# The second feed-forward's way down as seven block products, with tokens on the partitions

## The chip, the cores and the metric

The kernel is one decoder layer in float32 on one core of a Trainium2 chip. The metric is the device time of one execution in microseconds (us). The engines are named as in the profile: PE (TensorE: matrix products into the accumulator banks), PEld (its weight loads, which overlap the products), DVE (VectorE), ACT (ScalarE), POOL (GpSimd) and SP (SyncE, here only an issuer of transfers). Every engine takes its instructions in one fixed order, and a transfer issued from ACT or POOL stands in that engine's order too.

## The reference, cut to what matters

```python
def swiglu(h, w_gu, w_down):
    gu = h @ w_gu
    g, u = jnp.split(gu, 2, axis=-1)
    return (jax.nn.silu(g) * u) @ w_down          # the product this case is about
...
    f = swiglu(rmsnorm(h, ffn2_pre_g[l]), ffn2_w_gu[l], ffn2_w_down[l])
    h = h + 0.5 * rmsnorm(f, ffn2_post_g[l])      # the layer's last two lines
return h
```

There are 1024 tokens, the model width is 1024 and the inner width 2816, which is 22 inner tiles of 128. The product down is activations (1024 tokens x 2816) times `w_down` (2816 x 1024). After it come a norm over each token's 1024 values, a gain, and the addition of the residual `h`.

## The kernel before

All stages run one after the other on one core: a first feed-forward, a mixer (state-space part and attention), cross attention, and the second feed-forward (`ffn2`), which is the stage that changes. Float32 products are made of three passes (`mm3`, lines that all appear as L137): each operand is split into a high part rounded to the product's type (a cast on ACT, L248) and the low rest (a subtraction, L250, on DVE or POOL), and high x high, high x low and low x high are accumulated. One pass is a product of 128x128 (the loaded weight) by 128x512.

Tokens stand in two halves of 512 (`hh`), the model width in two halves (`dh`).

**The way up** (`up_phase`): inner tiles f = 0 to 2 are plain (12 projections of 24 passes). From f = 3 on, `seven(f)` computes a tile for both token halves by seven block products (a 2x2 block scheme) of 12 passes each; their inputs are sums of blocks of the normed residual (S, B21, B12: made once, in `steps` and `last`, from tiles `blk` that POOL loads by L683) and sums of weight blocks (L748 on POOL into `wc`, then split into a ring of `whi`/`wlo`/`blk` slots). The finished tile is stored to DRAM (`store`, L666, on ACT's queue): `act_d[j][hh][:, k]` holds inner tile 2j + k.

**The way down** (`down_phase`, then `last_rows`): plain products, 22 inner tiles x 2 token halves x 2 width halves x 4 blocks of 128 x 3 passes = 1056 passes. For the first token half the weights are the loaded operand and the result has the width on the partitions (`out_a`, transposed by the host); its norm needs column sums and a row broadcast by PE (`post`, `rms_cols`, `rms_rows`: tiles `ms`, `acc`, `cpost`, `rpost`). For the second half the tokens are on the partitions (`out_b`) and `last_rows` takes norm and residual block by block, with transposes of the residual (L140). Four banks at a time are filled from two inner tiles, then added into `F` by DVE (L501, L503). Weight rests are made by DVE, activation rests by POOL. Raw data come through four `wraw`/`raw2` buffers (512 KB each, `load`, L601, on SP's queue).

**Order.** PE's order is the program's. `self.later` holds actions with a due time on `self.clock`, an estimate of PE's time that grows with every pass; when PE's program passes the due time the action's instructions are traced. `kp` keeps an instruction behind the one traced before it on its engine; `urgent` gives priority. Other than that, a planner sets each engine's order when the kernel is built. Pools of one phase lie where pools of the phase before lay, so a first use waits for the old tile's last reader.

## Time and profile before

| | |
|---|---|
| median of 3 runs | 2786.47 us (2780.77 to 2788.60) |
| the profiled execution | 2785.41 us, its span 2783.6 us |
| granted TensorE clock, mean | 0.986 |
| busy: PE, PEld, DVE, ACT, POOL | 96%, 79%, 68%, 48%, 34% |
| second feed-forward's seven-product part | from 2153.97 to 2527.13 us of the span |
| second feed-forward's way down | from 2527.13 us to the end |

A row of the view by windows has the stretch, its length, the busy time and the instructions of each engine, the granted clock, the share of time that the transfer engines were busy, and GB/s. A timeline row has the start, the duration, the engine, the line, the operation and its operands (out<-in), how many were merged, and in brackets the idle time before it with what ended it. A row of the groups by line has the busy time, the mean duration in ns, and the idle time before. Overlapping matmuls show durations longer than their spacing, so PE's rate is read from starts.

### The profile page before, as it was taken

Reading aid. Unit: us, or ns where it says so; the run is one execution under the profiler, and the core shown is the slowest. Engines: PE = TensorE matmul, PEld = TensorE weight load, DVE = VectorE, ACT = ScalarE, POOL = GpSimd, SP = SyncE. Lnnn points to the kernel's source line nnn. Section 1 sums busy time; section 2 is a strip of 40 time slices with the busy share of each in tenths; the row PEclk is TensorE's granted clock in tenths of the full one; section 3 lists DMA queues with packets and bytes.
Section 4 is the critical chain, followed back from the end, with each engine's and each line's share of the span. In section 5 each row is a group of like instructions: output and inputs, shape, how many; then the busy total and the mean of one; then the engine's idle time right before and its main releaser. Section 6 shows DMA issues by size and latency. Waiting matters only on the chain.

```text
span 2783.6 us, 36828 instructions
## 1 busy us (share of the span) xinstructions
PE 2672.7 (96%) x12966; PEld 2202.3 (79%) x12966; DVE 1883.5 (68%) x2685; ACT 1338.5 (48%) x2409; POOL 941.2 (34%) x1027
## 2 busy tenths in 40 slices
PE   8899999999999999999999989999999999999998
PEld 6788888777777788887788787777878788888887
DVE  6787886346667674888888886665457755556656
ACT  6444444435245563666666655354555433332223
POOL 2555554324314351000000143532134645543222
PEclk9999999999999999999999999999999999999999
DMA  5588888874532225333333446544257322224332
GB/s 189 188 268 277 290 264 300 281 274 151 198 121 76 76 83 194 102 94 101 106 96 104 147 136 219 181 134 155 99 174 246 120 81 91 75 85 150 138 121 99
DMA packets 181913, 437.38 MB, mean 157 GB/s; under 512 B 21728, under 2 KB 30816, under 8 KB 181728
## 3 DMA queue, kind: packets, MB, share of 16 engines
q1 hardware_dynamic: 153312, 359.51, 39.6%
q0 software_dynamic: 15744, 52.44, 5.5%
q10 hardware_dynamic: 12672, 23.07, 2.2%
q8 instruction: 102, 1.67, 0.3%
q14 instruction: 83, 0.68, 0.1%
HBM read 300.72 MB, written 113.25 MB: 149 GB/s over the span
## 4 chain that ended last, share of the span: by engine, by line
PE 70%; DVE 12%; issue 6%; ACT 5%; DMA 5%; POOL 1%; SPq 0%; DVEq 0%; ACTq 0%; POOLq 0%
PE mm L137 37%; PE dn L137 26%; DVE nb L1644 2%; PE z L137 2%; PE tr L140 1%; DVE be L1648 1%; PE y L137 1%; PE ms L137 1%; ACT nb L1639 1%; PE ms L140 1%; DVE wlo L250 1%; DVE F L405 1%; PE seg L137 1%; ACT be L1639 1%; DVE F L401 1%
## 5 line engine op out<-in xcount | busy, mean ns | idle before, releaser
L137 PE MATMUL mm<-xh,whi 128*128 128x512 f32 x1356 | 541.7, 410 | 19.1 <-ACT xh L255 7.0
L137 PE MATMUL mm<-xh,wlo 128*128 128x512 f32 x1316 | 508.8, 395 | 0.7 <-ACT xh L248 0.3
L137 PE MATMUL mm<-xl,whi 128*128 128x512 f32 (+1 forms) x1254 | 494.3, 394 | 3.8 <-DVE xl L250 3.4
L137 PEld LDWEIGHTS mm<-xh,whi 128*128 128x128 f32 x1356 | 258.5, 191 | 66.7 <-ACT xh L248 8.1
L137 PEld LDWEIGHTS mm<-xh,wlo 128*128 128x128 f32 x1316 | 249.8, 190 | 57.7 <-ACT xh L248 1.6
L137 PEld LDWEIGHTS mm<-xl,whi 128*128 128x128 f32 x1254 | 239.7, 191 | 41.6 <-DVE xl L250 6.1
L1644 DVE TENSOR_TENSOR_SCAN nb<-nb,begin 128x128 f32<-128x128 f32 (+7 forms) x128 | 179.4, 1402 | 35.2 <-ACT nb L1639 35.1
L248 ACT CAST whi<-wraw 128x1024 fp32r<-128x1024 f32 (+1 forms) x110 | 98.1, 892 | 133.3 <-PE mm L137 75.6
L1643 POOL MEMSET nb<- 128x1 f32 x128 | 12.6, 98 | 366.6 <-DVE be L1648 345.1
L1639 ACT ACTIVATE nb<-z,scale 128x128 f32<-128x128 f32 (+2 forms) x192 | 111.8, 582 | 47.5 <-PE z L137 37.3
L137 PE MATMUL dn<-xh,wlo 128*128 128x512 f32 x364 | 126.6, 393 | 0.0
L137 PE MATMUL dn<-xh,whi 128*128 128x512 f32 x356 | 123.8, 393 | 0.3 <-DVE F L503 0.3
L250 DVE TENSOR_TENSOR wlo<-wraw,whi 128x1024 fp32r<-128x1024 f32 x62 | 82.3, 1327 | 56.2 <-ACT whi L248 55.9
L1639 ACT ACTIVATE be<-z,scale 128x128 f32<-128x128 f32 (+2 forms) x192 | 111.6, 582 | 0.0
L1648 DVE TENSOR_TENSOR be<-be,nb 128x128 f32<-128x128 f32 (+7 forms) x128 | 103.6, 809 | 11.5 <-ACT v L248 0.5
L361 POOL TENSOR_TENSOR acc<-acc,sq 128x512 f32<-128x512 f32 x42 | 58.6, 1396 | 148.0 <-ACT sq L359 147.9
L748 POOL TENSOR_TENSOR wc<-wraw,raw 128x512 f32<-128x512 f32 x58 | 84.3, 1453 | 67.1 <-DVE blk L250 22.1
L748 POOL TENSOR_TENSOR wc<-raw,wraw 128x512 f32<-128x512 f32 x56 | 83.2, 1485 | 52.7 <-DVE blk L250 19.2
L137 PE MATMUL dn<-xh,blk 128*128 128x512 f32 x312 | 100.8, 389 | 0.0
L137 PE MATMUL mm<-ath,v 128*128 128x256 f32 x320 | 86.5, 293 | 5.3 <-DVE ev L1745 4.3
L670 ACT ACTIVATE ft<-ft 128x512 f32<-128x512 f32 x88 | 55.5, 631 | 64.2 <-DVE ft L669 63.0
L250 POOL TENSOR_TENSOR hl<-raw,hl 128x512 fp32r<-128x512 f32 x28 | 38.1, 1369 | 137.1 <-ACT hl L248 137.1
(515 smaller groups left out, 7045.8 us busy)
## 6 DMA issues: line engine op xcount, KB each, us to landing
whi<-dwhi SPq DMA_DIRECT2D x78, 512.0 KB, 3.4
wlo<-dwlo SPq DMA_DIRECT2D x78, 512.0 KB, 4.4
wraw<-in_w_gu SPq DMA_DIRECT2D x44, 512.0 KB, 4.0
act<-ft ACTq DMA_DIRECT2D x88, 256.0 KB, 3.5
raw<-in_w_gu SPq DMA_DIRECT2D x38, 512.0 KB, 4.2
wraw<-in_w_dn SPq DMA_DIRECT2D x33, 512.0 KB, 4.2
raw<-in_w_dn SPq DMA_DIRECT2D x31, 512.0 KB, 4.4
xl<-h POOLq DMA_DIRECT2D x48, 256.0 KB, 4.3
```

The lines of the kernel that those rows point to most:

```text
L137: self._pe(self.nc.tensor.matmul(out, lhsT, rhs, start=start, stop=stop, skip_group_check=self.more), cost)
L140: self._pe(self.nc.tensor.transpose(out, src, self.ident if ident is None else ident), 109.0)
L248: self.kp(self.nc.scalar.copy(hi, src))
L250: (eng or self.nc.vector).tensor_tensor(out=lo, in0=src, in1=hi.bitcast(F32), op=ALU.subtract)
L361: self.kp(eng.tensor_tensor(out=accs[i % 2], in0=accs[i % 2], in1=sq, op=ALU.add))
L401: nc.vector.scalar_tensor_tensor(out=F, in0=F, scalar=self.par(gname, d), in1=r, op0=ALU.mult, op1=ALU.mult)
L405: self.kp(nc.vector.tensor_tensor(out=F, in0=F, in1=self.XL[hh][d], op=ALU.add))
L670: nc.scalar.activation(t, t, AF.Silu)
L748: nc.gpsimd.tensor_tensor(out=t, in0=a, in1=b, op=op)
L1639: nc.scalar.activation(o[:, s0:s1], z[:, 0:n], AF.Sigmoid, scale=sc[:, k, i : i + 1])
L1644: nc.vector.tensor_tensor_scan(out=nb[:, 0:Wd][:, ::-1], data0=nb[:, 0:Wd][:, ::-1], data1=begin[:, S - Wd : S][:, ::-1], initial=0.0, op0 ...
L1648: nc.vector.tensor_tensor(out=be[:, 0:Wd], in0=be[:, 0:Wd], in1=nb[:, 1 : Wd + 1], op=ALU.mult)
```

## The change

The way down of the second feed-forward is written as a 2x2 block scheme too. Token halves, halves of the inner width (even and odd inner tiles) and width halves form the blocks; seven block products of 11 inner tiles x 4 token blocks x 3 passes take the place of eight: 924 passes. Each runs over all its 11 inner tiles into four banks (512 width columns each), one per block of 128 tokens. Products 1 to 3 go on accumulating into the banks of product 0, with a copy or an addition into `F` between them. For each inner tile a fetch loads one activation block (256 KB) and one or two weight blocks, combines the weight blocks on POOL, and splits both operands on ACT and DVE. Weight blocks (1,1) and (0,0) are loaded once and stay in tiles that held the normed residual.

The five sums of activations that the scheme needs are made during the way up: when the four blocks of a pair of inner tiles are stored, POOL loads them again, DVE makes five sums, and ACT's queue stores these to DRAM (`act_sums`). The ring of weight blocks on the way up goes from 11 to 10 slots, and its `wc` tiles go to the other pool.

All tokens now stand on the partitions in the result: norm, gain and residual follow `last_rows` for both halves, with 64 transposes in place of 32; the column sums and row broadcast of `post` are no longer called here. The first half is finished during products 5 and 6, its stores issued by POOL; the second half's `dh` = 0 blocks get square sums and gain during product 6, and each block of tokens is ended behind its last bank. The residual is loaded by POOL as before (16 loads), from product 3 on.

The removed functions stand above. The diff, cut to its core:

```diff
     def ffn2(self, wgu, wdn, gpre, gpost, out):
         tc = self.tc
         with self.pools("f2", ["r"], []) as (rw, dnp):
-            self.rows = True
             act_d, bank, load = self.ffn(dnp, rw)
             plain = [self.wsrc("gu2", i) for i in range(2 * PLAIN)]
             with tc.tile_pool(name=self.nm("up"), bufs=1, reuse_waits="tile") as sp, \
                     tc.tile_pool(name=self.nm("ub"), bufs=1, reuse_waits="tile") as sp2:
-                self.up_phase(sp, sp2, wgu, gpre, act_d, bank, load, plain, (4, 3, 5))
+                xs_d = self.up_phase(sp, sp2, wgu, gpre, act_d, bank, load, plain, (4, 3, 4), rw)
             with tc.tile_pool(name=self.nm("dl"), bufs=1, reuse_waits="tile") as sp, \
                     tc.tile_pool(name=self.nm("dr"), bufs=1, reuse_waits="tile", side="right") as fp:
-                self.fp, self.ep = fp, sp
+                self.rw = rw
                 self.new_F(fp, fp)
-                self.down_phase(sp, wdn, act_d, bank, load, gpost, out)
+                self.down_rows(sp, wdn, act_d, xs_d, out.rearrange("(t p) d -> t p d", p=P))
 
...
+        xs_d, stored = {}, [0] * (NFF // 2)
+        spare = [] if begin else [self.xl(hh, F32) for hh in range(2)]
         def store(f, hh, t):
             o = act_d[f // 2][hh][:, f % 2, :]
             self.later.append((self.clock + 4500, lambda: self.kp(nc.scalar.dma_start(out=o, in_=t))))
+            stored[f // 2] += 1
+            if stored[f // 2] == 4 and not begin:
+                act_sums(f // 2, self.clock + 8000)
+        def act_sums(j, t0):
+            x = {}
+            names = ("a11", "a21", "a12", "a22")
+            def load(n):
+                if n == "a22":
+                    x[n] = self.t(self.tp, [P, H], F32, "dg", bufs=1)
+                else:
+                    x[n] = self.t(rw, [P, H], F32, "cb", bufs=3)
+                i = names.index(n)
+                self.kp(nc.gpsimd.dma_start(out=x[n], in_=act_d[j][i % 2][:, i // 2, :]))
+            def combine(n, out, a, b, op):
+                if out is None:
+                    out = spare[n == "s6"]
+                else:
+                    out = x[out]
+                self.kp(nc.vector.tensor_tensor(out=out, in0=x[a], in1=x[b], op=op))
+                x[n] = out
+            def put(n):
+                xs_d[n, j] = self.tc.dram_tile([P, H], F32, name=self.nm("xs"))
+                self.kp(nc.scalar.dma_start(out=xs_d[n, j], in_=x.pop(n)))
+            for i, n in enumerate(names):
+                at(t0 + 200 * i, load, n)
+            for i, (n, out, a, b, op) in enumerate((
+                ("s5", None, "a11", "a12", ALU.add), ("s6", None, "a21", "a11", ALU.subtract),
+                ("s1", "a11", "a11", "a22", ALU.add), ("s7", "a12", "a12", "a22", ALU.subtract),
+                ("s2", "a21", "a21", "a22", ALU.add),
+            )):
+                at(t0 + 5000 + 1200 * i, combine, n, out, a, b, op)
+                at(t0 + 7500 + 1200 * i, put, n)
 
...
-                u = self.t(sp, [P, H], F32, "wc", bufs=NWC)
+                u = self.t(sp2, [P, H], F32, "wc", bufs=NWC)
...
-                    t = self.t(sp, [P, 4, P], F32, "wc", bufs=NWC)
+                    t = self.t(sp if begin else sp2, [P, 4, P], F32, "wc", bufs=NWC)
...
         self.run_later(self.clock + 4600)
+        return xs_d
...
+    def down7(self, sp, wdn, act_d, xs_d, place, stay, finish):
+        seven = [
+            ("s5", ((1, 1),), None), ("s1", ((0, 0), (1, 1)), ALU.add), ("a22", ((1, 0), (0, 0)), ALU.subtract),
+            ("s7", ((1, 0), (1, 1)), ALU.add), ("a11", ((0, 1), (1, 1)), ALU.subtract), ("s2", ((0, 0),), None),
+            ("s6", ((0, 0), (0, 1)), ALU.add),
+        ]
+        there = set()
+        ready = []
+        def fetch(m, j):
+            x, ws, op = seven[m]
+            self.raws += 1
+            pool, tag = ((self.wp, "wraw"), (self.rw, "raw2"))[self.raws % 2]
+            raw = self.t(pool, [P, 2, H], F32, tag, bufs=2)
+            def block(b):
+                if b not in stay:
+                    nc.sync.dma_start(out=raw[:, 1], in_=wdn[j, b[1]][b[0]])
+                    return raw[:, 1]
+                t = stay[b][j]
+                if (b, j) not in there:
+                    there.add((b, j))
+                    nc.sync.dma_start(out=t, in_=wdn[j, b[1]][b[0]])
+                return t
+            w = [block(b) for b in ws]
+            k = {"a11": (0, 0), "a22": (1, 1)}.get(x)
+            nc.sync.dma_start(out=raw[:, 0], in_=xs_d[x, j] if k is None else act_d[j][k[0]][:, k[1], :])
+            if op is not None:
+                t = self.t(sp, [P, H], F32, "wc", bufs=3)
+                nc.gpsimd.tensor_tensor(out=t, in0=w[0], in1=w[1], op=op)
+                w = [t]
+            wt, xt = place(), self.t(sp, [P, 2, H], F32R, "hl", bufs=5)
+            if m == 0:
+                nc.scalar.activation(wt[:, 0], w[0], AF.Copy, scale=-1.0)
+                nc.vector.scalar_tensor_tensor(
+                    out=wt[:, 1], in0=w[0], scalar=-1.0, in1=wt[:, 0].bitcast(F32), op0=ALU.mult, op1=ALU.subtract
+                )
+            else:
+                self.split(wt[:, 0], wt[:, 1], w[0])
+            self.split(xt[:, 0], xt[:, 1], raw[:, 0])
+            ready.append((wt, xt))
+        order = [(m, j) for m in range(7) for j in range(NB)]
+        def take(n):
+            while order and len(ready) < n + 3:
+                fetch(*order.pop(0))
+            return [ready.pop(0) for _ in range(n)]
+        add = lambda out, a, b, op: nc.vector.tensor_tensor(out=out, in0=a, in1=b, op=op)
+        for m in range(7):
+            if m in (0, 4, 5, 6):
+                banks = [
+                    self.t(self.mmp, [P, H], F32, "mm") if m == 4 and i < 3 else self.t(self.dnp, [P, H], F32, "dn", bufs=4)
+                    for i in range(4)
+                ]
+            sizes = [2] + [1] * 7 + [2] if m < 6 else [2] + [1] * 5 + [4]
+            j = 0
+            for n, size in enumerate(sizes):
+                ops = take(size)
+                for i in range(4):
+                    c = slice(i * P, i * P + P)
+                    for jj, (w, x) in enumerate(ops):
+                        first = m in (0, 4, 5, 6) and j + jj == 0
+                        self.more = m in (1, 2, 3)
+                        self.mm3(
+                            banks[i], [(x[:, 0, c], x[:, 1, c], w[:, 0], w[:, 1])], first, j + jj == NB - 1
+                        )
+                        self.more = False
+                    if j + size < NB:
+                        continue
+                    ps = banks[i]
+                    (C11, C12), (C21, C22) = (self.F[hh][2 * i : 2 * i + 2] for hh in range(2))
+                    with self.urgent():
+                        if m == 0:
+                            nc.scalar.activation(C12, ps, AF.Copy, scale=-1.0)
+                        elif m == 1:
+                            nc.scalar.copy(C22, ps)
+                        elif m == 2:
+                            add(C21, ps, C22, ALU.subtract)
+                        elif m == 3:
+                            nc.scalar.copy(C11, ps)
+                        elif m == 4:
+                            add(C12, C12, ps, ALU.add)
+                        elif m == 5:
+                            add(C21, C21, ps, ALU.add)
+                            add(C22, C22, ps, ALU.subtract)
+                        else:
+                            add(C22, C22, ps, ALU.add)
+                    if m == 4:
+                        nc.gpsimd.tensor_tensor(out=C22, in0=C22, in1=C12, op=ALU.add)
+                    if m == 6:
+                        finish(m, i)
+                j += size
+            if m < 6:
+                finish(m, None)
+    def down_rows(self, sp, wdn, act_d, xs_d, out):
+        nc = self.nc
+        grow = self.t(sp, [P, D_MODEL], F32, "grow")
         dx = [self.t(sp, [P, 2, H], F32R, "dx", bufs=2) for _ in range(2)]
         nblk = [0]
                 return self.t(self.wp, [P, 2, H], F32R, ("whi", "wlo")[n % 2], bufs=3)
             return dx.pop(0) if dx else self.t(sp, [P, 2, H], F32R, "dx", bufs=2)
+        H_ = [[self.t(self.xp, [P, H], F32, f"xh{hh}{d}") for d in range(KT)] for hh in range(2)]
+        L_ = [[self.xl(hh, F32) for d in range(KT)] for hh in range(2)]
+        stay = {
+            (1, 1): H_[1][4:8] + L_[1][4:8] + H_[0][4:7], (0, 0): L_[0][4:8] + H_[0][7:8] + H_[1][0:4] + L_[1][0:2],
+        }
+        hs = [H_[0][0:4] + L_[0][0:4], H_[1][4:8] + L_[1][4:8]]
+        rh, sums = [], {}
+        def at(t, f, *args):
+            self.later.append((self.clock + t, lambda: f(*args)))
+        def fetch_h(hh, d):
+            self.kp(nc.gpsimd.dma_start(out=hs[hh][d], in_=self.h[hh][d]))
+        def shift(hh, tb):
+            xt = [self.t(self.mmp, [P, H], F32, "mm") for _ in range(2)]
+            for d in range(KT):
+                self.tr(xt[d // 4][:, (d % 4) * P : (d % 4 + 1) * P], hs[hh][d][:, tb * P : (tb + 1) * P])
+            return xt
+        def ssq(hh, tb, dh):
+            sq = self.t(self.tp, [P, H], F32, f"sq{dh}")
+            st = self.t(sp, [P, 1], F32, "st", bufs=16)
+            self.kp(nc.scalar.activation(sq, self.F[hh][2 * tb + dh], AF.Square, scale=self.C[hh][:, tb : tb + 1], accum_out=st))
+            if dh:
+                self.kp(nc.vector.tensor_tensor(out=st, in0=st, in1=sums[hh, tb], op=ALU.add))
+                self.kp(nc.scalar.activation(st, st, AF.Sqrt, scale=1.0 / D_MODEL, bias=self.eps))
+            sums[hh, tb] = st
+        def gain(hh, tb, dh):
+            F, r, g = self.F[hh][2 * tb + dh], rh[hh][:, tb : tb + 1], grow[:, dh * H : (dh + 1) * H]
+            if dh:
+                self.kp(nc.vector.scalar_tensor_tensor(out=F, in0=F, scalar=r, in1=g, op0=ALU.mult, op1=ALU.mult))
+            else:
+                self.kp(nc.scalar.activation(F, F, AF.Copy, scale=r))
+                self.kp(nc.gpsimd.tensor_tensor(out=F, in0=F, in1=g, op=ALU.mult))
+        def end(hh, tb, dh, xt):
+            F = self.F[hh][2 * tb + dh]
+            self.kp(
+                nc.vector.scalar_tensor_tensor(
+                    out=F, in0=F, scalar=sums[hh, tb], in1=xt[dh], op0=ALU.mult, op1=ALU.add
+                )
+            )
+        def store(hh, tb, dh, eng):
+            self.kp(eng.dma_start(out=out[4 * hh + tb, :, dh * H : (dh + 1) * H], in_=self.F[hh][2 * tb + dh]))
+        def root(hh, tb):
+            self.kp(nc.vector.reciprocal(sums[hh, tb], sums[hh, tb]))
+        def early(tb):
+            root(0, tb)
+            xt = shift(0, tb)
+            for dh in range(2):
+                end(0, tb, dh, xt)
+        def finish(m, tb):
+            if m == 2:
+                nc.sync.dma_start(out=grow, in_=self.ap["g_row"])
+                for hh in range(2):
+                    rh.append(self.t(sp, [P, 4], F32, f"rh{hh}"))
+                    nc.vector.tensor_scalar(out=rh[hh], in0=self.C[hh], scalar1=0.5, scalar2=None, op0=ALU.mult)
+                for d in range(KT):
+                    at(2500 * d, fetch_h, 0, d)
+            elif m == 4:
+                for tb in range(4):
+                    for dh in range(2):
+                        at(3000 + 12000 * tb + 1500 * dh, ssq, 0, tb, dh)
+                        at(6000 + 12000 * tb + 1500 * dh, gain, 0, tb, dh)
+                        at(14500 + 12000 * tb + dh, store, 0, tb, dh, nc.gpsimd)
+                    at(11000 + 12000 * tb, early, tb)
+                for d in range(KT):
+                    at(1000 + 2500 * d, fetch_h, 1, d)
+            elif m == 5:
+                for tb in range(4):
+                    at(3000 + 5000 * tb, ssq, 1, tb, 0)
+                    at(5000 + 5000 * tb, gain, 1, tb, 0)
+            elif m == 6:
+                if tb == 0:
+                    self.run_later(float("inf"))
+                last(tb)
+        def last(tb):
+            ssq(1, tb, 1)
+            gain(1, tb, 1)
+            root(1, tb)
+            xt = shift(1, tb)
+            for dh in range(2):
+                end(1, tb, dh, xt)
+                store(1, tb, dh, nc.sync)
+        self.down7(sp, wdn, act_d, xs_d, place, stay, finish)
...
-    ap["out"] = [
-        nc.dram_tensor(n, v, F32, kind="ExternalOutput").ap() for n, v in (("out_a", (KT, P, H)), ("out_b", (H, D_MODEL)))
-    ]
+    ap["out"] = nc.dram_tensor("out", (S, D_MODEL), F32, kind="ExternalOutput").ap()
```

More of the change, by code (lines that the diff above doesn't have):

```diff
@@ L611, in ffn1 @@
         rw, dnp = st.enter_context(self.pools("ff", [], ["r"]))
[L612 removed]
+        self.fp = rw
         act_d, bank, load = self.ffn(dnp, rw)
@@ L1085, in down_phase @@
-        for hh in range(2):
-            for bs in pairs:
-                xs = sum((take(acts, b, hh) for b in bs), [])
-                ws = []
-                for dh in range(2):
-                    ws.append(sum((take(weights, b, dh) for b in bs), []))
-                    if not hh or bs is pairs[0]:
-                        group(ws[dh], xs, dh, hh, False)
-            if hh == 0:
-                self.run_later(float("inf"))
-                self.post(0, gpost, self.C[0], out=out[0], step=1800)
```

134 lines of the change are left out of this document (4 added, 130 removed).

## The prediction

> **What bounds the kernel now.** I read the page's busy shares and chain of waits first, then busy times by windows over the stages that change, then timelines at their seams.
>
> ```profile
> PE 2672.7 (96%) x12966; PEld 2202.3 (79%) x12966; DVE 1883.5 (68%) x2685; ACT 1338.5 (48%) x2409; POOL 941.2 (34%) x1027
> PE 70%; DVE 12%; issue 6%; ACT 5%; DMA 5%; POOL 1%; SPq 0%; DVEq 0%; ACTq 0%; POOLq 0%
> PE mm L137 37%; PE dn L137 26%; DVE nb L1644 2%; PE z L137 2%; PE tr L140 1%; DVE be L1648 1%; PE y L137 1%; PE ms L137 1%; ACT nb L1639 1%; PE ms L140 1%; DVE wlo L250 1%; DVE F L405 1%; PE seg L137 1%; ACT be L1639 1%; DVE F L401 1%
> 2153.97:2182.00 28.03, 22.49 (x72) 15.63 (x71) 22.22 (x27) 14.37 (x25) 20.22 (x19) 0.76 0.44 143
> 2182.00:2527.13 345.13, 345.13 (x1525) 285.82 (x1523) 195.11 (x268) 117.59 (x197) 174.21 (x124) 1.00 0.26 84
> 2527.13:2700.00 172.87, 172.87 (x764) 143.22 (x763) 108.46 (x160) 45.24 (x77) 56.06 (x52) 1.00 0.42 142
> 2700.00:2757.00 57.00, 54.22 (x234) 44.00 (x233) 39.84 (x63) 19.65 (x34) 12.77 (x9) 0.97 0.34 117
> 2757.00:2784.00 27.00, 20.32 (x118) 17.52 (x116) 15.88 (x34) 10.89 (x26) 5.17 (x4) 0.97 0.27 96
> ```
>
> PE is busy 96% of the span and 63% of the chain is passes of L137 (37 + 26). From 2182.00 to 2700.00 PE's busy time equals the stretch to the hundredth: nothing else can shorten it, only fewer or quicker passes. PE idles in three places: at the start of the seven products (22.49 of 28.03, clock 0.76), around the first half's norm, and at the end. DVE there has 195.11 of 345.13 (57%), POOL 50%, ACT 34%.
>
> ```profile
> 2158.96 2.88 PE L137 MATMUL dn<-S,whi 128*128 128x512 f32 x12
> 2161.68 2.88 PE L137 MATMUL dn<-S,wlo 128*128 128x512 f32 x12
> 2527.13 2.00 PEld L137 LDWEIGHTS mm<-whi,whi 128*128 128x128 f32 x9
> 2775.57 0.88 PE L137 MATMUL dn<-dx,hl 128*128 128x256 f32 x6
> 2776.28 1.04 PE L140 MATMUL mm<-ident,xl 128*128 128x128 f32 x8
> ```
>
> Twelve passes start 2.72 us apart, 0.2267 us each. The way down starts at 2527.13 (call it E); its last pass ends at 2776.45 and the span at 2783.6, 7.15 later.
>
> **Term 1, the passes.** 1056 become 924: 132 x 0.2267 = 29.9 us off a stage where PE never waits, so all of it lies on the path.
>
> **Term 2, the first half's norm.** Its column sums and row broadcast go.
>
> ```profile
> 2730.58 1.32 PE L137 MATMUL ms<-small,acc 128*128 128x1 f32 x8 [1.33 <-DVE acc L363]
> 2732.34 3.30 PE L137 MATMUL dn<-whi,hl 128*128 128x512 f32 x9
> 2732.00:2735.50 3.50, 3.50 (x11) 2.74 (x12) 1.11 (x5) 0.30 (x1) 0.00 (x0) 0.63 0.02 5
> 2739.60 1.10 PE L137 MATMUL ms<-dg,onesr 128*128 128x512 f32 x2 [1.45 <-DVE dg L337]
> ```
>
> Removed: 1.32 + 1.10 of PE, idle time of 57.00 - 54.22 = 2.78, and 1.26 because nine passes took 3.30 instead of 9 x 0.2267 = 2.04 at a granted clock of 0.63: 6.5 us. As a check, 1056 x 0.2267 + 4 x 1.03 transposes + 6.5 + 6.3 after them makes 256.3, and 2783.6 - 2527.13 is 256.5.
>
> **Term 3, the transposes.** Eight cost 1.04 (the row at 2776.28). Four more sets for the first half stand in PE's order during products 5 and 6: +4.1 us. Their residual tiles are asked for two products (60 us) before. The first half's eight stores go from SP's queue to POOL's, each due 3.5 us after the final operations that it needs; behind a store that waits stand product 6's weight combinations, which run three inner tiles (8 us) ahead of PE. Cost 0 under that cover, some 3 us per late store without it.
>
> **Term 4, the end.** Before, the last block is 256 wide; now it is 512. Behind the last pass: addition, square sum with its read-out, root, reciprocal, two final operations, store.
>
> ```profile
> 2760.98 0.67 DVE L503 TENSOR_TENSOR F<-F,dn 128x512 f32<-128x512 f32 x1
> 2761.69 0.72 ACT L530 ACTIVATE sq<-F,cpre 128x512 f32<-128x512 f32 x1 [0.96 <-DVE F L503]
> 2762.32 0.18 ACT L530 ACTIVATION_READ_ACCUMULATOR sq<-F,cpre 128x1 f32 x1
> 2761.86 1.41 DVE L551 SCALAR_TENSOR_TENSOR F<-F,st,mm 128x512 f32<-128x512 f32 x2
> 2765.31 0.75 DVE L538 SCALAR_TENSOR_TENSOR F<-F,rh,grow 128x512 f32<-128x512 f32 x1
> 2778.07 0.29 ACT L545 ACTIVATE st<-st,small 128x1 f32<-128x1 f32 x1 [0.23 <-DVE st L532]
> 2778.39 0.16 DVE L548 RECIPROCAL st<-st 128x1 f32<-128x1 f32 x1
> 2778.69 1.66 DVE L551 SCALAR_TENSOR_TENSOR F<-F,st,mm 128x256 f32<-128x256 f32 x4
> ```
>
> 0.67 + 0.90 + 0.16 (sum of two columns, as the reciprocal) + 0.29 + 0.16 + 1.41 is 3.6; the gain (0.75, partly beside the root) and some five hops between engines (0.23 before the root) give 1.5; from the end of the last final operation (2778.69 + 1.66) to the span's end are 3.25. Sum 8.3 against 7.15: +1.1 us. DVE has 0.67 + 0.16 + 0.75 + 0.16 + 1.41 = 3.2 us per block and PE comes every 12 passes and 8 transposes, 3.76, so blocks don't pile up.
>
> **Term 5, feeding the way down.** Before, a 512 KB buffer served 24 passes or more; now each 12 passes need one fetch. No trace shows that rate, so I bound it.
>
> ```profile
> L250 DVE TENSOR_TENSOR wlo<-wraw,wlo 128x512 fp32r<-128x512 f32 x17 | 11.6, 684 | 9.5 <-ACT wlo L248 9.5
> L250 DVE TENSOR_TENSOR blk<-wc,blk 128x512 fp32r<-128x512 f32 x34 | 29.8, 877 | 9.0 <-ACT blk L248 8.7
> L748 POOL TENSOR_TENSOR wc<-raw 128x512 f32<-128x512 f32 x15 | 22.4, 1492 | 33.2 <-DVE blk L250 16.6 <-DVE wlo L250 8.3 <-DVE whi L250 8.3
> L248 ACT CAST hl<-raw 128x512 fp32r<-128x512 f32 x20 | 12.2, 620 | 22.3 <-PE dn L137 12.8 <-PE mm L137 8.5 <-DMA raw<-act 1.1
> 2535.67 0.33 SPq L601 DMA_DIRECT2D raw<-act  x1
> 2543.85 0.38 SPq L601 DMA_DIRECT2D raw<-in_w_dn  x1
> 2120.00:2130.00 10.00, 10.00 (x44) 7.89 (x43) 6.91 (x12) 6.75 (x12) 3.65 (x8) 1.00 0.97 357
> raw<-in_w_dn SPq DMA_DIRECT2D x14, 512.0 KB, 4.5
> ```
>
> Per 2.72 us: ACT two casts, 1.24; DVE two rests, 1.37 alone or 1.75 beside POOL (mean 877), plus 0.25 of additions; POOL one combination in five of seven products, 1.49; SP at most three issues, 1.1. Transfers: 512 KB, 193 GB/s, and 294 while residual loads run beside (256 KB per 2.6 us); 357 was moved at 2120. All engines have room. Latency: one buffer's cycle at the start of the way down went from its issue at 2535.67 to the next issue into the same kind of buffer at 2543.85, 8.2 us, with two casts and two POOL rests in it. Four buffers give one fetch per 2.05 us, under 2.72. Lower bound 0. Upper bound: a cycle of 12.3 us eats up the gain (below). I take 2 us, near the lower bound, for the banks handed over between products and DVE's two additions per bank after product 5 (8 x 0.68 beside the rests, in the 8.2 us until the last of the four banks is needed again). The first weight blocks land in tiles of the normed residual that the last tile's first seven-product operand holds until E - 6 x 2.72, 16.3 us before they are wanted, 4.5 of it for the landing: 0.
>
> **Term 6, the sums beside the way up.** Each pair of inner tiles (168 passes, 38.1 us) gets four POOL issues of 0.53 (the row of eight at 2156.88 below), five DVE additions of 0.68 and five ACT issues of 0.33 (as SP's at 2535.67). DVE goes from 57% to 66%, POOL from 50 to 56%, ACT from 34 to 38%; traffic grows by 11 x 9 x 256 KB.
>
> ```profile
> 2488.23 1.67 POOL L748 TENSOR_TENSOR wc<-raw 128x512 f32<-128x512 f32 x1 [4.15 <-DVE blk L250]
> 2524.63 0.39 PE L137 MATMUL dn<-xh,whi 128*128 128x512 f32 x1
> 2528.34 2.86 ACTq L666 DMA_DIRECT2D act<-ft  x2
> act<-ft ACTq DMA_DIRECT2D x2, 256.0 KB, 2.4
> ```
>
> What hides it is the stock of weight blocks: POOL makes the last one at 2488.23, PE uses it from about 2524.6, 36 us later. A ring of 10 takes 2.7 of this. If a POOL load waits for its stored tile, weight combinations stand behind it; if a DVE sum waits, additions out of the banks do, and with seven banks PE sees that after two products, 5.4 us. I take 0 there; without that cover each pair would pay a wait of some 3 us, 30 in all. The last pair's sums fall into product 0: store issued by E + 4.1 (2528.34 + 2.86), landed 2.4 later at E + 6.5, reloaded by about E + 12, summed at the due time of 13.0 by the clock, out at E + 16.3, landed at E + 19.6; SP, which waits for it, loads the tile by E + 23 and it is split by E + 24.6. PE wants it at 10 x 2.72 = E + 27.2: 2.6 us to spare. Behind SP's wait stand product 1's first loads, wanted at E + 29.9, there at about E + 26.6. Cost 0, at worst 5.
>
> **Term 7, the start of the seven products.** Here nothing hides a delay.
>
> ```profile
> 2156.88 4.26 POOL L683 DMA_DIRECT2D blk<-h  x8
> 2158.96:2165.57 6.61, 6.17 (x28) 4.80 (x26) 3.12 (x5) 1.97 (x4) 4.51 (x7) 1.00 0.86 311
> 2169.45 0.79 PE L137 MATMUL mm<-xh,whi 128*128 128x512 f32 x1 [3.49 <-ACT xh L248]
> ```
>
> PE waits 3.49 for B12, whose residual tiles POOL asked for only at 2156.88, behind weight combinations. The first pair's sums come due at 2151 to 2162: four POOL issues (2.2 us) ahead of these eight, 2.3 MB more beside transfers that already run at 311 GB/s, and 3.4 us of additions on a DVE that is busy 22.22 of 28.03 us. The stall costs 11.4 already: 19 tiles x 84 passes x 0.2267 are 361.8, and from 2153.97 to E are 373.16. The sums can fall into gaps that are there, and the new order of POOL could as well ask for B12's tiles sooner (lower bound -3); or they delay B12 by issue, transfer and addition in turn (2.2 + 2 + 3.4, about 8). I take 3, near the POOL issues alone, since these stand for certain on that queue.
>
> The row at 2732.00 also bears on term 2: 1.33 us without work and eight passes one column wide brought the clock to 0.63. A rule of the Trainium skill (TensorE: Matmul & The Clock Gate, "What's actually happening") would have the clock halve only after an idle window of about 3.4 us. By that rule the 1.26 of slow passes is no cost of the norm and would not be saved, and the sum would come to 2761; I go by the row.
>
> **Sum.** -29.9 - 6.5 + 4.1 + 1.1 + 2 + 0 + 3 = -26.2. From the profiled execution, 2785.41, to 2759.2; the median of the runs stands 1.1 higher: **2760 us**.
>
> **Rivals.**
> A, the sum: 2760, own range 2752 (term 5 at 0, term 7 at -3) to 2768 (term 6 at 5, term 7 at 6).
> B, fed too late in places: the order of engines is fixed at build time, and a combination on POOL, a cast and a rest stand one behind the other; where residual loads run beside (products 3 and 5), the cycle grows past 10.9 us, to 12 say, and 22 fetches cost 0.3 each plus clock losses of 1.3 for some: +10, 2770. For it: no row shows such a rate; against it: five `hl` tiles let splits run four inner tiles ahead.
> C, the B12 start: sums and B12's chain stand in one order on DVE, ACT waits to store a sum while a scale stands behind; term 7 at 8, and cold passes for 6 us longer, +5 more: 2770.
> D, the other side: the fetch is the bound throughout. It has 77 fetches; the gain of 26.2 is gone at 0.34 us each, a fetch per 3.06 us, a buffer cycle of 12.3 us. At 13.5 us it is 3.38 per fetch: 77 x 0.66 = 50 more, 2810. For it: the landing alone is 4.5, and two loads, POOL, ACT and DVE follow in order; against it: 8.2 us measured with the same count of operations.
> The number of passes is fixed by the code, so the change does what it says.
>
> **How the numbers follow.** A 0.62, B 0.12, C 0.14, D 0.10, something between D and no gain 0.02. Within 0.3% (about what runs of this kernel can tell from no change, 8 us) is 2778 to 2795. Faster is A, B and C: 0.88; the same 0.02; slower 0.10. The range is 2751 (terms 4 and 5 at 0, term 7 at -3) to 2775 (B or C, with 5 of term 6).
>
> **What would show it.** Passes of the way down: 924, PE full in products 0 to 6, E to the end about 227 us (209.5 + 8.2 + 2 + 7.4). PE's wait on `xh` before 2182 longer than 3.49 by up to 3 speaks for term 7, by more for C. PE waits on `hl` or `wc` rests, or SP waits on `raw` buffers with PE idle, speak for B or D; a wait at E + 27 for the last pair's sum would make term 6 wrong. Ends of blocks more than 3.8 us apart, or over 8.3 behind the last pass, would make term 4 wrong.

## The result, and the profile after

After: 2789.23 us median (2787.26 to 2797.20, 20 runs); before, with it: 2783.58 us (2778.19 to 2790.51, 20 runs). The ratio is 1.0024, with a 95% interval of 1.0016 to 1.0031: a little slower, 29 us over the forecast. The profiled execution took 2788.44 us, its span 2786.7.

The page of the kernel after: busy shares, and the chain of waits by engine and by line.

```profile
PE 2658.3 (95%) x12844; PEld 2182.4 (78%) x12844; DVE 1911.9 (69%) x2701; ACT 1368.1 (49%) x2483; POOL 1002.2 (36%) x1095
PE 7%; DMA 2%; DVE 2%; POOL 1%; issue 1%; ACT 1%; DVEq 0%; POOLq 0%; ACTq 0%; SPq 0%
PE dn L137 5%; PE mm L137 2%; DMA raw<-in_w_dn 1%; POOL wc L1009 1%; DVE hl L250 1%; DMA wraw<-in_w_dn 0%; DVE F L1030 0%; ACT hl L248 0%; ACT whi L248 0%; DVE F L1136 0%; POOL ft L789 0%; DMA cb<-act 0%; ACT dx L248 0%; DVE F L1128 0%; ACT sq L1119 0%
```

The passes are gone (12844 products on PE for 12966), and PE is busy 14.4 us less. But the chain, which was PE's, now has in it the loads of `in_w_dn`, the weight combination of L1009 and the rests of L250: the way down waits for its fetches. Chain shares are of the whole span and add up to 14%, so it was followed through the last 390 us or so.

The view by windows, over the same stages as before (the way up now ends at 2535.86, which is 2540.04 less a wait of 4.18):

```profile
2153.97:2182.00 28.03, 20.27 (x69) 14.00 (x69) 25.82 (x31) 12.63 (x22) 18.43 (x18) 0.80 0.56 191
2182.00:2535.86 353.86, 351.45 (x1533) 289.11 (x1532) 228.41 (x320) 113.46 (x200) 191.84 (x159) 0.99 0.44 154
2535.86:2700.00 164.14, 152.88 (x644) 122.29 (x645) 91.69 (x123) 69.45 (x124) 73.40 (x57) 0.97 0.55 175
2700.00:2787.00 87.00, 74.48 (x346) 60.89 (x344) 67.57 (x96) 40.91 (x86) 43.47 (x39) 0.93 0.48 163
```

No window is full any more. And PE's timeline, the rows with the long waits; the first row is the first pass of the seven products (2158.96 before), the last one the last passes:

```profile
2160.68 1.55 PE L137 MATMUL dn<-S,whi 128*128 128x512 f32 x6
2171.70 0.80 PE L137 MATMUL mm<-xh,whi 128*128 128x512 f32 x1 [4.71 <-ACT xh L248]
2175.78 0.80 PE L137 MATMUL mm<-xh,whi 128*128 128x512 f32 x1 [1.71 <-ACT xh L248]
2203.57 4.25 PE L137 MATMUL mm<-S,whi 128*128 128x512 f32 x12 [1.92 <-DVE e L768]
2540.04 1.65 PE L137 MATMUL dn<-whi,hl 128*128 128x512 f32 x3 [4.18 <-ACT hl L248]
2637.78 1.62 PE L137 MATMUL dn<-wlo,hl 128*128 128x512 f32 x3 [5.43 <-DVE F L1030]
2739.97 0.94 PE L137 MATMUL dn<-whi,hl 128*128 128x512 f32 x3 [4.28 <-DVE F L1030]
2777.71 0.85 PE L137 MATMUL dn<-whi,hl 128*128 128x512 f32 x3
```

The way up (first pass of the seven products to the end of its last pass) took 2535.86 - 2160.68 = 375.2 us for 2527.13 - 2158.96 = 368.2: +7.0. The way down took 250.8 for the 227 predicted: 24 too long. Its three large waits are 13.9 us, the small ones 2.2, and passes behind them run at half clock. Two of the large ones stand at seams (products 2 to 3 and 5 to 6), where the banks' additions (L1030) come late.

Why they come late is read from the other engines' timelines before the first of these seams, here merged in order of time:

```profile
2628.12 0.43 SPq L1006 DMA_DIRECT2D raw<-xs  x1
2630.53 1.43 POOL L1009 TENSOR_TENSOR wc<-raw,xh 128x512 f32<-128x512 f32 x1 [1.70 <-DMA raw<-in_w_dn]
...
2631.99 0.62 ACT L248 CAST whi<-wc 128x512 fp32r<-128x512 f32 x1 [1.99 <-POOL wc L1009]
2632.51 0.61 ACT L248 CAST hl<-raw 128x512 fp32r<-128x512 f32 x1
...
2634.38 0.43 SPq L1006 DMA_DIRECT2D raw<-xs  x1
2636.95 0.69 DVE L1030 TENSOR_TENSOR F<-dn,F 128x512 f32<-128x512 f32 x1
...
2638.72 0.61 ACT L248 CAST hl<-raw 128x512 fp32r<-128x512 f32 x1
2640.65 0.68 DVE L250 TENSOR_TENSOR hl<-raw,hl 128x512 fp32r<-128x512 f32 x1
```

Follow the fetch whose activation is asked for at 2628.12. Its weights are combined at 2630.53 and cast at 2631.99. ACT's next cast, `hl<-raw` at 2632.51, is not its own: that belongs to the fetch two before, whose buffer is free at 2633.93 and is filled again from 2634.00. Its own activation is cast at 2638.72, behind the weight cast of the fetch two later, and its buffer is free at 2641.33. So the loop issue, landing, combination, weight cast, activation cast of two fetches earlier, rest, next issue takes 6.25 us (2628.12 to 2634.38) and serves two fetches: one per 3.13 us, over PE's 2.72. All the while ACT's and DVE's orders are strict, so the first bank's addition stands at 2636.95 behind splits that wait for that loop. At the second seam the additions also stand behind last operations of the first half (L1136 at 2736.03); these rows don't tell apart what each of the two costs there.

### The profile page after: what moved, and what is told of

The parts are those of the page before. It is cut to its first block, busy times and chain, and to the rows that moved or that the text cites. A ratio compares the mean times of both kernels' runs of the same rounds, so it can differ in the third digit from the quotient of the medians.

```text
span 2786.7 us, 37015 instructions
## 1 busy us (share of the span) xinstructions
PE 2658.3 (95%) x12844; PEld 2182.4 (78%) x12844; DVE 1911.9 (69%) x2701; ACT 1368.1 (49%) x2483; POOL 1002.2 (36%) x1095
## 5 line engine op out<-in xcount | busy, mean ns | idle before, releaser
L137 PE MATMUL dn<-xh,wlo 128*128 128x512 f32 x396 | 137.2, 393 | 0.5 <-DMA wlo<-dwlo 0.5
L250 DVE TENSOR_TENSOR wlo<-wraw,whi 128x1024 fp32r<-128x1024 f32 x62 | 82.4, 1330 | 56.4 <-ACT whi L248 56.1
L248 ACT CAST wlo<-wc 128x512 fp32r<-128x512 f32 x81 | 50.2, 620 | 108.5 <-POOL wc L1009 32.1
L250 DVE TENSOR_TENSOR wlo<-wc,wlo 128x512 fp32r<-128x512 f32 x81 | 66.7, 824 | 52.6 <-ACT wlo L248 48.9
L250 DVE TENSOR_TENSOR whi<-wc,whi 128x512 fp32r<-128x512 f32 x83 | 68.7, 828 | 45.4 <-ACT whi L248 29.9
```

Of the source, the lines that this page charges most:

```text
L137: self._pe(self.nc.tensor.matmul(out, lhsT, rhs, start=start, stop=stop, skip_group_check=self.more), cost)
L248: self.kp(self.nc.scalar.copy(hi, src))
L250: (eng or self.nc.vector).tensor_tensor(out=lo, in0=src, in1=hi.bitcast(F32), op=ALU.subtract)
```

## The experiments

The theory: every saved pass is there, and is paid back (1) by this fetch loop, because five `hl` tiles leave two of four raw buffers holding waiting activations; (2) by the first activation casts at the start of the way down; (3) by the sums of activations on the way up, through where they stand on POOL, DVE and ACT. Rivals: loads or POOL as such set the pace; seams alone are at fault; the sums cost by their amount, or the smaller weight ring does.

| kernel | median us (runs) | ratio to before, 95% | way up | way down |
|---|---|---|---|---|
| before | 2783.58 (20) | 1 | 368.2 | 256.5 |
| after | 2789.23 (20) | 1.0024 (1.0016 to 1.0031) | 375.2 | 250.8 |
| e1_first_x | 2788.52 (11) | 1.0019 (1.0008 to 1.0029) | 375.4 | 254.1 |
| e2_seven_hl | 2766.62 (5) | 0.9936 (0.9924 to 0.9947) | 376.6 | 230.6 |
| e3_late_pair0 | 2790.71 (11) | 1.0026 (1.0014 to 1.0038) | 374.2 | 255.0 |
| e4_no_sums | 2785.09 (12) | 1.0000 (0.9991 to 1.0008) | 367.6 | 253.2 |
| e5_six_raw | 2768.95 (6) | 0.9948 (0.9934 to 0.9962) | 376.7 | 231.7 |
| e6_six_hl | 2771.15 (6) | 0.9955 (0.9941 to 0.9969) | 374.4 | 237.0 |
| e7_first_x_seven_hl | 2760.84 (6) | 0.9912 (0.9895 to 0.9930) | 375.7 | 227.1 |
| e8_later_sums | 2762.60 (5) | 0.9920 (0.9905 to 0.9935) | 376.2 | 226.6 |
| e9_sums_apart | 2762.81 (5) | 0.9925 (0.9910 to 0.9940) | 375.3 | 225.8 |
| e10_sums_one_pair_later | 2755.59 (4) | 0.9907 (0.9890 to 0.9923) | 367.3 | 228.7 |

Way up and way down come from the profiled execution of each, as worked out above (a wait at the seam between the two counts to the way down). They tell small edits apart better than the medians, since some 10 us of difference between two executions are there before this stage: its first `S` pass starts at 2153.8 (e9) to 2164.5 (e5). Executions that share the way up's code still differ by 2.3 us in it (374.4 to 376.7: after, e1, e2, e5, e6, e7). The ratio is to runs of before taken along with each kernel, whose medians lie at 2782.19 to 2785.36.

**e1, the first activations of the way down.**

```diff
-            wt, xt = place(), self.t(sp, [P, 2, H], F32R, "hl", bufs=5)
+            wt = place()
+            xt = place() if m == 0 and j < 2 else self.t(sp, [P, 2, H], F32R, "hl", bufs=5)
```

> Edit: in product 0 the first two activation tiles are split into slots of the ring that has the weights, as before the change; the rest stays. Theory (the first activation casts of the way down wait because their own tiles lie where late tiles of the way up lay, and so end behind two stores on ACT): PE's wait of 4.18 us at 2540.04 on the cast of `hl` falls to under 1 us, the half-clock passes behind it go, the time falls by 5 to 6 us, to about 2784. Rival (the data themselves come late, loaded behind the stay blocks on SP's queue): the wait stays over 3 us and the time within 2 us of 2789.2. The waits of 5.43 and 4.28 us at the seams of products 2-3 and 5-6 stay in both cases.

The wait went, the time did not: 2788.52. PE's timeline of this kernel:

```profile
2563.98 0.50 PE L137 MATMUL dn<-whi,hl 128*128 128x512 f32 x1 [1.58 <-DVE hl L250]
...
2605.42 0.96 PE L137 MATMUL dn<-whi,hl 128*128 128x512 f32 x3 [1.63 <-ACT F L1060]
...
2641.41 1.65 PE L137 MATMUL dn<-wlo,hl 128*128 128x512 f32 x3 [1.76 <-DVE F L1031]
2675.96 0.73 PE L137 MATMUL mm<-dx,hl 128*128 128x512 f32 x2 [2.16 <-ACT hl L248]
```

The seams keep their waits (4.69 and 3.69 us), as expected, and the gain is paid back by new waits at 2564, 2605, 2641 and 2676. Neither expectation foresaw that. The reading, which e7 tests: where a pace bounds a stage, a stall taken out ahead of it comes back later.

**e2, seven `hl` tiles.**

```diff
-            wt, xt = place(), self.t(sp, [P, 2, H], F32R, "hl", bufs=5)
+            wt, xt = place(), self.t(sp, [P, 2, H], F32R, "hl", bufs=7)
```

> Edit: seven tiles for split activations (`hl`) instead of five, nothing else. Theory (a split activation waits for a free `hl` tile, holds its raw buffer meanwhile, and ACT's order puts the weight cast of two inner tiles later in front of it, so that two fetches take 6.25 us and the additions of the next seam stand behind late splits): the waits at the seams 2-3 and 5-6 (5.43 + 0.83 and 4.28 + 0.90 us) fall below 1 us each, the fetches of products 2 to 6 come at PE's own 2.72 us, and with the half-clock passes behind both stalls 14 to 17 us go: 2772 to 2775. Rival D of the prediction, in the form that the transfers or POOL set the pace (landing 2.45, combination 1.3): the fetches stay 3.1 us apart, the seams' waits stay above 3 us each, and the time stays above 2783. The wait of 4.18 us at 2540 stays in both cases.

22.6 us less than after, more than the theory's 14 to 17; the waits at the seams fall to 0 and 0.23 us. Issues of three fetches in a row, then the view of waits from 2575 to 2700 us (engine, line, what it waited for: us, times, longest), first of this kernel:

```profile
2617.49 0.43 SPq L1006 DMA_DIRECT2D wraw<-xs  x1
2619.79 0.43 SPq L1006 DMA_DIRECT2D raw<-xs  x1
2622.37 0.43 SPq L1006 DMA_DIRECT2D wraw<-xs  x1
...
ACT hl L248 <- PE dn L137: 60.8, 35, 3.6
```

and of the kernel after:

```profile
POOL wc L1009 <- DMA wraw<-in_w_dn: 32.8, 14, 4.0
ACT wlo L248 <- POOL wc L1009: 26.5, 12, 4.2
DVE wlo L250 <- ACT wlo L248: 23.6, 10, 3.6
...
ACT hl L248 <- PE dn L137: 5.5, 3, 2.7
```

Issues come 2.3 to 2.6 us apart in these rows. The waits are the clearest reading of the case. After, each engine of the loop waits for the one ahead of it, and only 5.5 us of ACT's waits are for PE. With seven tiles ACT waits for PE to free an `hl` tile, 35 times: PE is the slowest again. The same loads, combinations and additions run, so the transfers, POOL and the seams' additions were not the bound by themselves. The Trainium skill (Perfetto Trace Analysis, "Optimization Strategy") has it that a gap that repeats on the engine that should be full can mean too few buffers; here PE showed two long gaps in products 1 to 6, at seams, and the gap that repeated was SP's, 3.13 us between issues.

**e5, six raw buffers, and e6, six `hl` tiles.**

```diff
-            pool, tag = ((self.wp, "wraw"), (self.rw, "raw2"))[self.raws % 2]
+            pool, tag = ((self.wp, "wraw"), (self.rw, "raw2"), (sp, "raw3"))[self.raws % 3]
```

> Edit: six raw buffers instead of four, five `hl` tiles as in the changed kernel (the same 8 KB more as with seven `hl` tiles). Theory (two of the four raw buffers are held by activations that wait for an `hl` tile, so one fetch loop of 6.25 us serves two fetches): with six buffers the loop serves four, the pace is PE's, and most of the 22.6 us that seven `hl` tiles gave comes here too: 2766 to 2772, seams' waits below 1.5 us. Rival (it is the free `hl` tile that PE waits for, raw buffers have nothing to do with it): fetches still 3.1 us apart, waits at the seams 2-3 and 5-6 above 3 us each, 2785 to 2790.

e6 has `bufs=6` in the line of e2.

> Edit: six `hl` tiles instead of five. Theory: the split of an activation then stands behind the weight cast of one tile later, not two; the loop of about 6.25 us serves three fetches, 2.1 us each, under PE's 2.72, so one tile more is enough: 2766 to 2770 and seams' waits below 1 us. If instead every tile more gives a part of the gain (a stock that only lasts longer, with the pace as it was), the time lies half way, 2776 to 2780, and fetches stay about 3.1 us apart.

Both mend most of it, 20.3 and 18.1 us less than after. With six raw buffers, where the time and the seams' waits (0.38 us at most) came as the theory had them, the tiles that e2 added are missing and the gain comes all the same: it is the buffers held by waiting activations. One `hl` tile more is enough for the pace (issues 2.7 us apart); but one seam kept its wait, against the expectation, and the median lies 1.2 us above its range. DVE's and PE's timelines of e6:

```profile
2718.79 3.43 DVE L250 TENSOR_TENSOR dx<-wc,dx 128x512 fp32r<-128x512 f32 x1 [1.83 <-ACT dx L248]
...
2723.56 1.62 PE L137 MATMUL dn<-whi,hl 128*128 128x512 f32 x3 [5.00 <-DVE F L1030]
```

There the additions, from 2722.14 on, stand behind one rest that took 3.43 us where others take 0.7. Why it did is not shown.

**e7, e1 and e2 together.**

> Edit: seven `hl` tiles, and the first two activation tiles of product 0 in the weights' ring (the edit that alone gave 2788.5). Theory (the first stall was worth nothing alone because the fetch pace of products 2 to 6 took it back): with the pace mended the stall of 4.18 us and its half-clock passes count in full, 5 to 6 us: 2760 to 2762. Rival (the first stall is hidden by something else at the end as well): within 2 us of 2766.6.

5.8 us under e2, as the theory had it. The edit that was worth nothing under the slow pace counts in full once PE is the bound. Its way down, 227.1 us, is what the prediction's sum said (227); PE is busy there for 217.6 us, for 209.5 + 8.2.

**e3 and e4, the sums beside the way up.**

```diff
-                act_sums(f // 2, self.clock + 8000)
+                act_sums(f // 2, self.clock + (8000 if f > 1 else 53000))
```

> Edit: the sums of the first pair of inner tiles come due 45 us later by the program's clock, behind the start of the seven products; all other sums as they are. Theory (term 7: they delay B12 by what they take on POOL, DVE and the transfers): PE's idle time from 2160 to 2185 goes from 7.6 us back towards 5.5 and the time falls by 2 to 4 us, to 2785 to 2787. Rival (the planner's order of the start, or two fewer slots for weights, and not the sums, lengthened it): idle time still 7 us or more, time within 1 us of 2789. The DVE wait of 1.92 us at 2203.6, put down to the second pair's sums, stays in both cases.

e4 has no `act_sums`:

> Left out: all sums of activations beside the way up (their loads, additions and stores); the way down loads single activation blocks in their place, so its work and transfers stay the same and the output is not the reference's. It prices terms 6 and 7 together. Theory: the way up from 2154 to the start of the way down shrinks from 382 back to about 374 us (the B12 start 2 to 3, the wait at 2203.6 with its half clock about 4), and the time falls by 6 to 9 us, to 2780 to 2783. Rival (the longer way up comes from the ring of 10 weight slots, not the sums): the way up stays above 379 us and the time above 2787. The way down keeps its three waits of 4 to 5 us in both cases.

e3 brought B12's idle time from 7.6 to 6.1 us but new waits on `e`, the largest 1.21 at 2242, took it back: way up 374.2, a miss. e4 settled whose cost it is: without the sums, with the ring still at ten, the way up is 367.6, 7.6 us less. The median follows with 4.1 only, 2785.09, above the 2780 to 2783 expected.

How sums stop PE, in the timelines of DVE and POOL in the kernel after:

```profile
2196.78 0.58 POOL L602 DMA_DIRECT2D cb<-act  x1
...
2201.62 1.29 DVE L609 TENSOR_TENSOR xl<-cb,cb 128x512 f32<-128x512 f32 x2 [4.24 <-DMA cb<-act]
2202.83 0.68 DVE L768 TENSOR_TENSOR e<-sq,mm 128x512 f32<-128x512 f32 x1
```

Two sums wait 4.24 us on DVE for a load that POOL issued late; the addition into `e` stands behind them, and PE needs its bank at 2203.57.

**e8, e9, e10, other places for the same sums.** All are e7 with other due times, e8's and e9's as their expectations tell them; e10:

```diff
-                act_sums(f // 2, self.clock + 8000)
+                first = self.first = self.clock + 70000 if f < 2 else self.first
+                act_sums(f // 2, max(self.clock + 8000, first + 29300 * (f // 2)))
...
-                at(t0 + 5000 + 1200 * i, combine, n, out, a, b, op)
-                at(t0 + 7500 + 1200 * i, put, n)
+                t = t0 + (7000 + 2000 * i if j < NFF // 2 - 1 else 5000 + 1200 * i)
+                at(t, combine, n, out, a, b, op)
+                at(t + 2500, put, n)
```

> Edit: as the run before it, and the sums beside the way up come due later by the program's clock: the first pair's 53 us, the last pair's not, all others 6 us. Theory (a DVE sum whose loads have not landed stands ahead of the additions out of the banks, and the first pair's sums lengthen the wait for B12; leaving all sums out made the way up 7.6 us shorter): the waits on `e` at 2202 (1.9 to 2.6 us, with half clock behind it) go, B12 costs 6 instead of 7.6 us, and the time falls by 4 to 6 us, to 2755 to 2757. Rival (the sums cost the way up by their traffic or their share of DVE, not by where they stand): within 2 us of the run before it.

> Edit: as e7_first_x_seven_hl, and DVE's sums stand elsewhere in its order: the loads of a pair come due 4 us later, its five sums 9 us behind those and 2.4 us apart (so that they stand behind the addition into `e`, one or two at a time, instead of four in a row ahead of it), the first pair's all between the second's and the third's; the last pair's stay. Number, traffic and engines of the sums are the same. Theory (it is the place in DVE's order that costs: a sum whose loads land later than the planner assumed holds the addition into `e`, and a run of four or five sums delays it; the later due times of the run before only moved that to 2223): the way up, from the first pass of the seven products to the first of the way down, falls from 375.7 to 368 to 370 us, no wait on `e` over 0.5 us, and the time lies at 2753 to 2756. Rival (the sums cost by their number or traffic, wherever they stand): way up at 374 or more, time 2759 to 2763.

> Edit: as e7_first_x_seven_hl, and the sums of each pair come due when the pair has been in DRAM for long: the first 70 us after its store by the program's clock, the following every 29.3 us (never before 8 us behind the store), five sums 2 us apart; the last pair's as they were. So no load waits for a store on POOL, and none stands in the first two of the seven-product tiles, where the stock of weight blocks is still being made. Theory (the sums cost only where a load, a copy or the addition into `e` stands behind one of them that waits; run before: 1.91 + 2.33 us at 2230 to 2236, all in the first five tiles): the way up, first pass of the seven products to the first of the way down, falls from 375.3 to 367.5 to 369.5 us, and the time to 2752 to 2757. Rival (the sums cost 7 us by number or traffic): way up at 374 or more, new waits in other places, time 2758 to 2763.

(In e9's edit the sums come due 14 us behind a pair's first load, 9 us more than in e7.)

e8 and e9 missed: the way up stayed at 376.2 and 375.3, and both times came where the rival, a cost by amount, had them. But PE's waits stand in other places, e8 first, then e9:

```profile
2200.56 3.02 PE L137 MATMUL mm<-S,whi 128*128 128x512 f32 x12 [1.54 <-DVE e L768]
2223.11 5.49 PE L137 MATMUL dn<-S,blk 128*128 128x512 f32 x12 [3.21 <-DVE e L768]
```

```profile
2230.56 0.50 PE L137 MATMUL dn<-xh,wlo 128*128 128x512 f32 x1 [1.91 <-ACT sq L759]
2235.90 4.54 PE L137 MATMUL mm<-S,blk 128*128 128x512 f32 x12 [2.33 <-DVE e L769]
```

A later due time moved the waits; spreading the sums moved them again, to POOL, where a load waited for its store (`dg<-act`, issued at 2232.03 after 0.82 us) ahead of the subtraction of `sq` that `e` needs. e10 asks for a pair only when it has long been stored, and leaves out the first tiles, where the stock of weight blocks is still small. The view by windows of e10:

```profile
2182.00:2524.82 342.82, 342.82 (x1514) 283.97 (x1513) 249.18 (x319) 115.35 (x196) 195.33 (x160) 1.00 0.47 162
```

From 2182.00 to 2524.82 PE is full to the hundredth with all sums beside it. The way up is 367.3, as if there were none, so they cost by their place and not by their amount. The edit moves the loads, the first pair and the spacing of the sums at once, and which of these did it is not told apart. This kernel is faster than before and after: 2755.59 us, 0.9907 of before (0.9890 to 0.9923). It is not told apart from e7 by the medians' ratios, whose intervals overlap; it is by the way up.

## Why the prediction was wrong

- **Term 1** (29.9) and **terms 2 and 3** held, as far as their sum shows: with the feed mended the way down is 227.1 (e7) and 228.7 us (e10) for the 227 forecast.
- **Term 4** held in its size, by luck: the span ends 2786.70 - 2778.56 = 8.1 us behind the last pass, 8.3 predicted. But the last blocks' additions come at 2775.57 and 2779.54, 3.97 apart, over the 3.8 named, while PE's last passes of these blocks end 3.63 apart (2774.93 and 2778.56). So blocks do pile up: DVE's 3.2 us per block left out that DVE waits for ACT's square sum, 0.94 us in each block. The last addition starts 0.98 us behind its last pass, and the steps behind it took about as much less than forecast. DVE's timeline of the kernel after:

```profile
2779.54 0.68 DVE L1030 TENSOR_TENSOR F<-F,dn 128x512 f32<-128x512 f32 x1
2781.16 0.16 DVE L1121 TENSOR_TENSOR st<-st,st 128x1 f32<-128x1 f32 x1 [0.94 <-ACT sq L1119]
```

- **Term 5 is the step that failed**: "four buffers give one fetch per 2.05 us" and, against rival B, "five `hl` tiles let splits run four inner tiles ahead". It took the cycle of a buffer from the old kernel, 8.2 us, where there were eight `hl` tiles and the casts in that cycle waited for the load alone. Here there are five, and a raw buffer is held until PE frees an `hl` tile and ACT's order comes round. First ACT's row of the cycle before, then fetches of product 2 in the kernel after:

```profile
2540.12 1.14 ACT L248 CAST hl<-raw 128x512 fp32r<-128x512 f32 x2 [1.06 <-DMA raw<-act]
```

```profile
2587.59 0.42 SPq L1006 DMA_DIRECT2D raw<-act  x1
2590.72 0.42 SPq L1006 DMA_DIRECT2D wraw<-act  x1
...
2600.14 0.43 SPq L1006 DMA_DIRECT2D raw<-act  x1
```

  The buffer of 2587.59 is refilled at 2600.14: a cycle of 12.55 us, 3.14 per fetch. Rival D put the break-even at 12.3 and had a chance of 0.10; its mechanism was right in part: the pace is that slow only where POOL combines a block loaded into the raw buffer itself (products 2, 3, 4 and 6, 44 of 77 fetches). The time came out between no gain and D, which had 0.02. Term 5 was put at 2 us; the fetch pace cost 20 in the way down (250.8 against 230.6 in e2), and 24 with the next point (227.1 in e7).
- Also term 5: its last sentence costed the first weight blocks and not the first activations. These moved from the weights' ring into `hl` tiles, and their casts stood on ACT behind the last two stores of the way up: 4.18 us and its slow passes, 5.8 by e7. ACT's timeline of the kernel after (the bracket names `rh`, but that ended at 2539.06 and the stores were being issued until 2539.32):

```profile
2536.68 2.64 ACTq L586 DMA_DIRECT2D act<-ft  x2
2539.37 0.62 ACT L248 CAST hl<-raw 128x512 fp32r<-128x512 f32 x1 [2.80 <-DVE rh L1159]
```

- **Term 6** was put at 0 under the cover of the weight stock, with some 30 us without it. The danger named, "if a DVE sum waits, additions out of the banks do", is what happened, for the second pair above all (1.92 us and 12 passes at 4.25 us instead of 2.88; one more wait, at 2396.82, is 0.43); the last pair's sums were in time, as worked out.
- **Term 7** (+3): B12's idle time went from 5.4 (3.49 and four shorter waits) to 7.6 us (4.71, 1.71 and two), so +2.2 and slower passes. Terms 6 and 7 together measured 7.0 (after against before) to 8.4 us (e7 against e10), for 3.
- The sum of what was missed: 29 us. 22.6 (e2), 5.8 (e7) and about 5 (e10) undo it and 4 more. The 5 is the least sure of these: it is by the medians, and by the ratios, 0.9912 and 0.9907, it would be 1.4.

## What to carry to other kernels

A ring of buffers is worth only those that aren't held by data waiting for another ring: work out the cycle from issue to release with every engine's order in it, in the new kernel, before dividing by the number of buffers; and read who waits for whom, since in a stage that is fed too slowly the engines wait for the one ahead and hardly for PE. Test a suspected stall only once the pace behind it is mended, or its gain may be paid back and the stall look harmless. Extra work beside a full engine can cost by its place in the in-order queues: ask for its data only when they have long been there.

## What the runs showed of the hardware that wasn't expected

Short waits cost PE clock, but not always. Behind e8's wait of 1.54 us the clock stayed, behind its wait of 3.21 it fell; the windows right behind both, of e8:

```profile
2200.50:2204.00 3.50, 3.44 (x15) 2.87 (x16) 2.43 (x5) 0.63 (x1) 0.40 (x1) 1.00 0.46 173
2223.10:2228.00 4.90, 4.89 (x12) 3.83 (x13) 4.64 (x7) 1.68 (x3) 2.87 (x4) 0.50 0.69 239
```

In e10 it fell 1.5 us after PE had begun again behind a wait of 2.35 us; PE's timeline (three passes take 0.75 to 0.78 from start to start in the first two rows, 1.28 in the third):

```profile
2709.04 0.93 PE L137 MATMUL dn<-whi,hl 128*128 128x512 f32 x3 [2.35 <-DVE F L1033]
2709.82 0.95 PE L137 MATMUL dn<-wlo,hl 128*128 128x512 f32 x3
2710.57 1.48 PE L137 MATMUL dn<-whi,hl 128*128 128x512 f32 x3
2711.85 1.48 PE L137 MATMUL dn<-wlo,hl 128*128 128x512 f32 x3
```

That would fit a clock that is judged by a window which doesn't begin with the wait; no run here shows the window itself. The Trainium skill (TensorE: Matmul & The Clock Gate, "What's actually happening") has such a window, which runs free, and gives 3.4 us as its length; but its condition, that one window be idle, isn't needed here: 1.92 us of waiting in the kernel after, at 2203.57 (granted clock 0.69 over the next 4 us), and 2.35 in e10 were enough. So waits shorter than that length did cost clock, as the prediction took from its row.
